# Second-layer modulation in half tiles, later stores of low parts, casts on ScalarE: a diffusion step on one core

## The chip, the core and the metric

The kernel runs on one core of a Trainium2 chip. The metric is device time in microseconds for one execution of the whole program. Engines are named as in the profile: TensorE (PE for matmuls, PEld for its weight loads), VectorE (DVE), ScalarE (ACT), GpSimd (POOL) and SyncE (SP), which issues the DMA transfers. PSUM is the memory into which TensorE accumulates, SBUF the working memory of all engines.

## What is computed

The reference is one inference step of a small diffusion backbone: two layers over 128 context tokens and 1024 latent tokens, 1024 features wide. Every layer normalises its input, scales and shifts it by a modulation computed from a conditioning vector, mixes tokens, adds the result back with a gate, and does the same once more around a feed-forward block with a 3-tap convolution. Layer 0 mixes by neighbourhood attention and pooling, layer 1 by a convolution module. Cut to what matters here:

```python
for i in range(DEPTH):                                        # 2 layers
    mc = jnp.split(sc @ w_mod[i] + b_mod[i], N_MOD, axis=-1)  # six vectors of 1024, context
    ml = jnp.split(sl @ w_mod[i] + b_mod[i], N_MOD, axis=-1)  # the same, latent
    hl = rmsnorm(xl, norm_mix[i]) * (1 + ml[1]) + ml[0]
    # even layer: attention + pooling, w_out;  odd layer: conformer_conv
    xl = xl + ml[2] * yl
    hl = rmsnorm(xl, norm_ffn[i]) * (1 + ml[4]) + ml[3]
    xl = xl + ml[5] * conv_ffn(hl, ffn_w_in[i], ffn_conv_w[i], ffn_conv_b[i], ffn_w_out[i])
```

Everything is float32. `w_mod[1]`, the second layer's modulation weights, is 1024 x 6144 numbers, 25 MB.

## The kernel before

Activations are kept feature-major: 128 features on the partitions, 1154 token columns (128 context, 2 of padding, 1024 latent). To keep float32 accuracy every matmul is done as three: weight and activation are each split into a rounded high part (`hi`, type float32r) and the rest (`lo`), and `mm3` (L254) adds hi·hi, hi·lo and lo·hi in PSUM (L259, L261, L263). The token axis is cut in two parts, A (about 664 columns, two PSUM banks) and B (about 492, one bank), which go through each stage one after the other, so that vector work of one part runs beside the matmuls of the other.

A weight unit of 128 x 1024 is brought in by `wload` (L233, one 512 KB DMA on SP into one of two `wraw` tiles) and split by `wunit` (L238): ScalarE makes `whi` by a rounding copy (L247), POOL subtracts to get `wlo` (L249). `whi` and `wlo` have three tiles each after attention. In the first FFN of layer 0 (part A) each low part is also stored to DRAM (L251, `lowi` and `lowo`, 66 stores), so that part B can load it (L246) instead of computing it again.

`norm` (L390) makes the modulated input of a stage: squares on ScalarE, sums on VectorE (L401), a column sum on TensorE (L375), a rsqrt on POOL (L366), a broadcast by TensorE (L387), then for each of 8 feature tiles a multiply on VectorE (L414), scale and shift on ScalarE (L416), the cast to the high part on VectorE (L422) and the low part on POOL (L423). With `halo` the first two columns are copied from the other part's tiles (L421, on VectorE). The same cast stands in `conv_norm` (L1048) and where the attention output is read back from DRAM for the output projection (L1281, 16 casts, the first of them before attention has ended). `norm` runs six times in the trunk, which makes 48 casts and 32 halo copies.

`mod_beside` (L304) computes the second layer's modulation on VectorE, beside matmuls of layer 0. For each of three thirds it goes over 16 chunks of 128 x 1024 weights (512 KB): one DMA on SP into the single tile `mraw` (L310, L311), then four multiply-accumulates of 512 columns (L319, for the first chunks L317), two for each half. The DMA waits until the tile's last reader is done. `keep_in_program_order` fixes the order among these. After 16 chunks a small matmul (L325) and `mod_spread` bring the result into place. The generator yields after each half; `trunk` pulls it four times (MS) after each output-projection tile of part A, and 1.1 times after each step of the first FFN. The residual add `x += gate * psum` (L432) evicts the output matmuls from PSUM on VectorE; in the FFN ScalarE (L1082) and VectorE (L1083, L1085) evict.

The order of instructions on each engine is fixed when the program is built, from a simulated timeline and the order of the program; on the chip each engine and each DMA queue then works strictly in that order. Transfers that the steps name: v rows are read back from DRAM in 128 loads (`vr`, L780), x and the attention output (`cat`) through SP as well.

```python
rv = raw[:, x * 512:(x + 1) * 512]                 # L313, in mod_beside: half of the one mraw tile
acc, c = accs[4 * s + 2 * u + x], self.sc[:, k, s:s + 1]
i = nc.vector.scalar_tensor_tensor(acc, rv, c, acc, op0=ALU.mult, op1=ALU.add)
```

Of the kernel before, what the change touches and what calls it, by code (L numbers as in the profile page):

```python
# [9 lines left out]
F32 = mybir.dt.float32  # L10
F32R = mybir.dt.float32r
AF = mybir.ActivationFunctionType
# [7 lines left out]
P = 128  # L20
# [11 lines left out]
H = 8  # L32
# [156 lines left out]
class Kern:  # L189
    def __init__(self, ctx, tc, ins, outs):  # L190
        self.tc = tc
        self.nc = tc.nc
        self.i = ins
        self.o = outs
        self.uid = 0
        self.pstack = None
        self.bg = []
        self.due = 0.0

    def nm(self, s):  # L200
# [32 lines left out]
    def wload(self, src):  # L233
        raw = self.wp.tile([P, 1024], F32, tag="wraw", name=self.nm("wraw"), bufs=2)
        self.nc.sync.dma_start(raw, src)
        return raw

    def wunit(self, src, raw=None, eng=None, keep=None, kept=None):  # L238

        nc = self.nc  # L240
        if raw is None:
            raw = self.wload(src)
        hi = self.wp.tile([P, 1024], F32R, tag="whi", name=self.nm("whi"), bufs=self.wbufs)
        lo = self.wp.tile([P, 1024], F32R, tag="wlo", name=self.nm("wlo"), bufs=self.wbufs)
        if kept is not None:
            nc.sync.dma_start(lo.bitcast(F32), kept)  # L246
        nc.scalar.activation(hi, raw, AF.Copy)  # L247
        if kept is None:
            (eng or nc.gpsimd).tensor_tensor(lo, raw, hi.bitcast(F32), op=ALU.subtract)  # L249
        if keep is not None:  # L250
            nc.sync.dma_start(keep, lo.bitcast(F32))  # L251
        return hi, lo

    def mm3(self, part, ps, whi, wlo, xhi, xlo, off, start, stop):  # L254
# [49 lines left out]
    def mod_beside(self, l, m, wp, ap, tag, ev):  # L304

        nc = self.nc
        accs = [ap.tile([P, UW], F32, tag=tag, name=self.nm("modacc"))[:, :512] for _ in range(8)]
        for k in range(KT):
            for u in range(2):
                raw = wp.tile([P, 1024], F32, tag="mraw", name=self.nm("mraw"), bufs=1)  # L310
                nc.sync.dma_start(raw, self.i["wmod"][l, m, k, :, u * 1024:(u + 1) * 1024])  # L311
                for x in range(2):
                    rv = raw[:, x * 512:(x + 1) * 512]  # L313
                    for s in range(2):
                        acc, c = accs[4 * s + 2 * u + x], self.sc[:, k, s:s + 1]
                        if k == 0:
                            i = nc.vector.tensor_scalar(acc, rv, c, None, op0=ALU.mult)  # L317
                        else:
                            i = nc.vector.scalar_tensor_tensor(acc, rv, c, acc, op0=ALU.mult, op1=ALU.add)  # L319
                        self.tc.keep_in_program_order(i)  # L320
                    yield
        ps = self.psa.tile([P, 512], F32, tag="aux", name=self.nm("modps"))
        for s in range(2):
            for g in range(4):
                nc.tensor.matmul(ps[32 * g:32 * g + 32, :], self.one[:, 1 - s:33 - s], accs[4 * s + g],  # L325
                                 start=s == 0, stop=s == 1)
        yield
        self.mod_spread(l, m, ps, ev, self.psa, "aux")
        yield
# [60 lines left out]
    def norm(self, part, xs, g, sh, H, tp, halo=None, gap=1):  # L390

        nc = self.nc
        W, c0, c1 = part.w, part.c0, part.c1
        acc = None
        for k in range(KT):
            sq = tp.tile([P, self.tw], F32, tag="ft", name=self.nm("sq"))
            nc.scalar.activation(sq[:, :W], xs[k][:, c0:c1], AF.Square)
            if acc is None:
                acc = sq
            else:  # L400
                nc.vector.tensor_tensor(acc[:, :W], acc[:, :W], sq[:, :W], op=ALU.add)  # L401
            yield
        ms = self.psa.tile([P, 512], F32, tag="aux", name=self.nm("ms"))
        st = part.toks()
        self.colsum(ms, (acc,), self.cst("on"), [o - c0 for o in st])
        r = self.rsqrt(ms[:, :len(st)], len(st))
        for _ in range(gap):
            yield
        rb = self.pstile()
        self.bcast(part, rb, r)  # L410
        off = c0 - H.base
        for k in range(KT):
            t = tp.tile([P, self.tw], F32, tag="ft", name=self.nm("nt"))
            nc.vector.tensor_tensor(t[:, :W], part.ps(rb), xs[k][:, c0:c1], op=ALU.mult)  # L414
            for s, a, b in part.streams(c0, c1):
                nc.scalar.activation(t[:, a - c0:b - c0], t[:, a - c0:b - c0], AF.Identity,  # L416
                                     bias=sh[:, k, s:s + 1], scale=g[:, k, s:s + 1])
            hi, lo = H.new()
            if halo is not None:
                for d, x in ((hi, halo.hi[k]), (lo, halo.lo[k])):  # L420
                    nc.vector.tensor_copy(d[:, 0:off], x[:, H.base - halo.base:c0 - halo.base])  # L421
            nc.vector.tensor_copy(hi[:, off:off + W], t[:, :W])  # L422
            nc.gpsimd.tensor_tensor(lo[:, off:off + W], t[:, :W], hi[:, off:off + W].bitcast(F32), op=ALU.subtract)  # L423
            H.hi.append(hi)
            H.lo.append(lo)
            yield
# [574 lines left out]
    def conv_norm(self, part, accs, H, sp, tp):  # L1001

        nc = self.nc
        A = part.c0 == 0
        W = part.w
        l0 = NCTX + CP
        sh = (lambda c: c if c < NCTX else c - L0 + l0) if A else (lambda c: c - part.c0)
        n = sh(part.c1 - 1) + 1
        st = [sh(c) for c in part.toks()]
        ms = self.psa.tile([P, 512], F32, tag="aux", name=self.nm("cmu"))  # L1010
        self.colsum(ms, (accs.pop(),), self.cst("on"), st)
        m = self.cp.tile([P, 24], F32, tag="mean", name=self.nm("mean"), bufs=1)
        nc.vector.tensor_copy(m[:, :len(st)], ms[:, :len(st)])
        for _ in range(NM):
            yield
        mb = self.pstile()
        self.bcast(part, mb, m)
        vs = None
        for k in range(KT):
            for _, pv, a, b in part.pieces(mb, part.c0, part.c1):  # L1020
                av = accs[k][:, sh(a):sh(a) + b - a]
                nc.vector.tensor_tensor(av, av, pv, op=ALU.subtract)
            sq = tp.tile([P, self.tw], F32, tag="ft", name=self.nm("csq"))
            nc.scalar.activation(sq[:, :n], accs[k][:, :n], AF.Square)
            if vs is None:
                vs = sq
            else:
                nc.gpsimd.tensor_tensor(vs[:, :n], vs[:, :n], sq[:, :n], op=ALU.add)
            yield
        ms = self.psa.tile([P, 512], F32, tag="aux", name=self.nm("cvar"))  # L1030
        self.colsum(ms, (vs,), self.cst("on"), st)
        r = self.rsqrt(ms[:, :len(st)], len(st))
        for _ in range(GC):
            yield
        rb = self.pstile()
        self.bcast(part, rb, r)
        for k in range(KT):
            t = tp.tile([P, self.tw], F32, tag="ft", name=self.nm("ct"))
            for _, pv, a, b in part.pieces(rb, part.c0, part.c1):
                av = accs[k][:, sh(a):sh(a) + b - a]  # L1040
                nc.vector.tensor_tensor(t[:, a - part.c0:b - part.c0], av, pv, op=ALU.mult)
            if A:
                nc.gpsimd.memset(t[:, NCTX:L0], 0.0)
            for _, a, b in part.streams(part.c0, part.c1):
                tv = t[:, a - part.c0:b - part.c0]
                nc.scalar.activation(tv, tv, AF.Silu, bias=self.par("lnb", k), scale=self.par("lng", k))
            hi, lo = H.new()
            nc.vector.tensor_copy(hi[:, :W], t[:, :W])  # L1048
            nc.gpsimd.tensor_tensor(lo[:, :W], t[:, :W], hi[:, :W].bitcast(F32), op=ALU.subtract)
            H.hi.append(hi)  # L1050
            H.lo.append(lo)
            yield
# [184 lines left out]
    def trunk(self):  # L1237
        tc, nc, I, cp = self.tc, self.nc, self.i, self.cp
# [10 lines left out]
        with ExitStack() as st:  # L1249
# [15 lines left out]
            for k in range(KT):  # L1265
                x = xp.tile([P, T], F32, name=f"x_{k}")
# [7 lines left out]
            for part, Hc in ((OA, mkA()), (OB, mkB(OB.c0))):  # L1274
                Hc.order = order
                tiles = {}
                for k in order:
                    c = ft.tile([P, self.tw], F32, tag="ft", name=self.nm("cat"))
                    nc.sync.dma_start(c[:, :part.w], self.cat[k][:, part.c0:part.c1])
                    hi, lo = Hc.new()  # L1280
                    nc.vector.tensor_copy(hi[:, :part.w], c[:, :part.w])  # L1281
                    nc.gpsimd.tensor_tensor(lo[:, :part.w], c[:, :part.w], hi[:, :part.w].bitcast(F32),
                                            op=ALU.subtract)
                    tiles[k] = (hi, lo)
# [207 lines left out]
```

## Time and profile before

| | |
|---|---|
| median of 3 runs | 2737.82 us (2730.47 to 2738.35) |
| the profiled execution | 2735.89 us, span of its trace 2734.1 us |
| mean granted TensorE clock | 0.986 |
| TensorE busy | 2643.0 us, 97% of the span |
| VectorE, ScalarE, POOL busy | 1690.7, 1071.8, 1265.3 us |
| DMA | 341 MB, 125 GB/s on average |

The span runs from the first to the last instruction; the execution's own time has 1.8 us around it. A busy TensorE is not one at its peak, as its matmuls overlap. The granted clock is the share of full speed that the chip let TensorE run at; it has two levels, 2.4 and 1.2 GHz. A row of a timeline gives start, duration, engine, line, operation and, in brackets, the engine's idle time before and what ended it.

### The profile page before, as it was taken

How to read it: one execution, taken by the hardware profiler on the slowest of the kernel's cores; microseconds unless marked ns; L12 is line 12 of the kernel's file. 1: busy time of each engine (PE TensorE's matmuls, PEld its weight loads, DVE VectorE, ACT ScalarE, POOL GpSimd, SP SyncE). 2: the span in 40 equal slices, each digit the busy share in tenths (PEclk: the TensorE clock that was granted, in tenths of full speed). 3: DMA queues.
4: the chain of work that ended last, by engine and by line, in shares of the span. 5: the costliest groups of instructions: out<-in, count | busy, mean ns of one | idle time of the engine just before them, and what ended most of it. 6: DMA issues, size and time to landing. Idle time of an engine off the chain costs nothing.

```text
span 2734.1 us, 38719 instructions
## 1 busy us (share of the span) xinstructions
PE 2643.0 (97%) x15108; PEld 2384.5 (87%) x15108; DVE 1690.7 (62%) x2568; ACT 1071.8 (39%) x1631; POOL 1265.3 (46%) x752
## 2 busy tenths in 40 slices
PE   8999998998999999999999999999999999999999
PEld 6688886787999988978999789989999999888887
DVE  3236878568666767764897864569965444544444
ACT  3325665523422222235555353455333322433332
POOL 1323444254423323215555253699756544645553
PEclk9999998998999999999999999999999999999999
DMA  7622224354445545644444554232222222433232
GB/s 264 198 75 68 55 54 131 124 181 138 153 149 193 184 163 171 201 161 141 144 145 133 177 172 135 74 99 70 66 82 70 78 79 76 123 93 93 93 94 91
DMA packets 130902, 341.16 MB, mean 125 GB/s; under 512 B 44960, under 2 KB 50208, under 8 KB 130720
## 3 DMA queue, kind: packets, MB, share of 16 engines
q1 hardware_dynamic: 130720, 338.68, 38.8%
q8 instruction: 120, 1.97, 0.3%
q14 instruction: 62, 0.51, 0.1%
HBM read 291.97 MB, written 46.67 MB: 124 GB/s over the span
## 4 chain that ended last, share of the span: by engine, by line
PE 75%; DVE 14%; DMA 7%; ACT 2%; issue 1%; POOL 1%; SPq 0%; POOLq 0%; DVEq 0%; ACTq 0%
PE mm L259 13%; PE mm L261 13%; PE mm L263 13%; PE mn L259 8%; PE mn L261 7%; PE mn L263 7%; DMA mraw<-in_wmod_dram 4%; DVE modacc L319 4%; PE mm L449 2%; DVE x L432 1%; DVE dacc L987 1%; PE O L879 1%; PE ms L479 1%; PE qps L629 1%; PE qps L631 1%
## 5 line engine op out<-in xcount | busy, mean ns | idle before, releaser
L249 POOL TENSOR_TENSOR wlo<-wraw,whi 128x1024 fp32r<-128x1024 f32 x280 | 686.9, 2458 | 915.1 <-ACT whi L247 767.2
L247 ACT ACTIVATE whi<-wraw 128x1024 fp32r<-128x1024 f32 x348 | 364.5, 1056 | 763.7 <-PE mm L261 374.8
L259 PE MATMUL mm<-h,whi 128*128 128x332 f32 (+6 forms) x2208 | 558.5, 324 | 9.2 <-DVE x L432 8.7
L263 PE MATMUL mm<-h,wlo 128*128 128x332 f32 (+6 forms) x2208 | 559.9, 324 | 0.1
L261 PE MATMUL mm<-h,whi 128*128 128x332 f32 (+6 forms) x2208 | 559.5, 324 | 0.0
L259 PEld LDWEIGHTS mm<-h,whi 128*128 128x128 f32 x2208 | 382.5, 189 | 22.5 <-issue 10.4
L263 PEld LDWEIGHTS mm<-h,wlo 128*128 128x128 f32 x2208 | 381.2, 189 | 12.7 <-issue 0.8
L261 PEld LDWEIGHTS mm<-h,whi 128*128 128x128 f32 x2208 | 379.8, 189 | 11.0 <-issue 0.8
L987 DVE SCALAR_TENSOR_TENSOR dacc<-u,params,dacc 128x661 f32<-128x661 f32 (+1 forms) x344 | 285.4, 830 | 7.5
L432 DVE SCALAR_TENSOR_TENSOR x<-mm,mod,x 128x128 f32<-128x128 f32 (+7 forms) x408 | 210.7, 560 | 101.0 <-PE mm L263 87.1
L259 PE MATMUL mn<-h,whi 128*128 128x494 f32 (+1 forms) x672 | 262.8, 391 | 2.9 <-DVE x L432 2.9
L261 PE MATMUL mn<-h,whi 128*128 128x494 f32 (+1 forms) x672 | 262.3, 390 | 0.0
L263 PE MATMUL mn<-h,wlo 128*128 128x494 f32 (+1 forms) x672 | 260.8, 390 | 0.0
L319 DVE SCALAR_TENSOR_TENSOR modacc<-mraw,sc,modacc 128x512 f32<-128x512 f32 x168 | 167.8, 1053 | 67.5 <-DMA mraw<-in_wmod_dram 67.5
L1083 DVE SCALAR_TENSOR_TENSOR facc<-mm,params,facc 128x663 f32<-128x663 f32 (+3 forms) x92 | 81.9, 891 | 206.2 <-ACT facc L1082 206.0
L1083 DVE SCALAR_TENSOR_TENSOR facc<-mn,params,facc 128x493 f32<-128x493 f32 (+1 forms) x84 | 62.0, 738 | 207.8 <-ACT facc L1082 207.7
L259 PE MATMUL mm<-fh,whi 128*128 128x332 f32 (+2 forms) x720 | 173.5, 321 | 15.7 <-DVE x L432 13.3
L263 PE MATMUL mm<-fh,wlo 128*128 128x332 f32 (+2 forms) x720 | 171.5, 318 | 0.3 <-POOL wlo L249 0.3
L261 PE MATMUL mm<-fl,whi 128*128 128x332 f32 (+2 forms) x720 | 171.6, 318 | 0.0
L969 POOL TENSOR_TENSOR acc<-acc,tap 128x508 f32<-128x508 f32 (+1 forms) x104 | 151.1, 1455 | 38.0 <-ACT tap L968 31.8
L432 DVE SCALAR_TENSOR_TENSOR x<-mn,mod,x 128x510 f32<-128x510 f32 (+1 forms) x168 | 120.6, 737 | 64.7 <-PE mn L263 64.1
L1095 POOL TENSOR_TENSOR facc<-facc,facc 128x494 f32<-128x494 f32 (+2 forms) x66 | 91.2, 1382 | 149.9 <-DVE facc L1085 149.9
(227 smaller groups left out, 4555.6 us busy)
## 6 DMA issues: line engine op xcount, KB each, us to landing
wraw<-in_fi_dram SPq DMA_DIRECT2D x176, 512.0 KB
mraw<-in_wmod_dram SPq DMA_DIRECT2D x96, 512.0 KB
wraw<-in_fo_dram SPq DMA_DIRECT2D x88, 512.0 KB
wraw<-in_pw_dram SPq DMA_DIRECT2D x48, 512.0 KB
lowi<-wlo SPq DMA_DIRECT2D x44, 512.0 KB
wlo<-lowi SPq DMA_DIRECT2D x44, 512.0 KB
lowo<-wlo SPq DMA_DIRECT2D x22, 512.0 KB
wlo<-lowo SPq DMA_DIRECT2D x22, 512.0 KB
```

Of the source, the lines that this page charges most:

```text
L247: nc.scalar.activation(hi, raw, AF.Copy)
L249: (eng or nc.gpsimd).tensor_tensor(lo, raw, hi.bitcast(F32), op=ALU.subtract)
L259: mm(pv, whi, xhi[:, a:b], start=start, stop=False)
L261: mm(pv, whi, xlo[:, a:b], start=False, stop=False)
L263: mm(pv, wlo, xhi[:, a:b], start=False, stop=stop)
L319: i = nc.vector.scalar_tensor_tensor(acc, rv, c, acc, op0=ALU.mult, op1=ALU.add)
L432: nc.vector.scalar_tensor_tensor(xd[:, a:b], pv, gate[:, d, st:st + 1], xd[:, a:b], op0=ALU.mult, op1=ALU.add)
L449: mm(ps[:, c, :n], w[:, s], x[k][:, o:o + n], start=a, stop=b)
L969: nc.gpsimd.tensor_tensor(acc[:, :n], acc[:, :n], p[:, :n], op=ALU.add)
L987: nc.vector.scalar_tensor_tensor(acc[:, :n] if t == NCK - 1 else pacc, u[:, t:t + n], wk(i, t), acc[:, :n] if t == side else pacc, op0=ALU ...
L1083: nc.vector.scalar_tensor_tensor(acc[:, 1:W], part.ps(ps, 0, W - 1), w(0), acc[:, 1:W], op0=ALU.mult, op1=ALU.add)
L1095: (nc.gpsimd if side or part.n == 1 else nc.vector).tensor_tensor(a[:, :W], a[:, :W], g[:, :W], op=ALU.mult)
```

## The change

Four edits. The modulation loads of `mod_beside` become halves of 128 x 512 (256 KB), each with its own DMA into one of three tiles. A low part is no longer stored by `wunit` itself: the store is noted and issued by the next `wload`, behind that load. The casts to the high part in `norm`, `conv_norm` and the read-back of the attention output, and the halo copies in `norm`, go from VectorE to ScalarE. Arithmetic and results stay the same.

```diff
@@ Kern.__init__
+        self.stores = []
@@ wload
         raw = self.wp.tile([P, 1024], F32, tag="wraw", name=self.nm("wraw"), bufs=2)
         self.nc.sync.dma_start(raw, src)
+        for dst, lo in self.stores:
+            self.nc.sync.dma_start(dst, lo)
+        self.stores = []
         return raw
@@ wunit
         if keep is not None:
-            nc.sync.dma_start(keep, lo.bitcast(F32))
+            self.stores.append((keep, lo.bitcast(F32)))
@@ mod_beside
-                raw = wp.tile([P, 1024], F32, tag="mraw", name=self.nm("mraw"), bufs=1)
-                nc.sync.dma_start(raw, self.i["wmod"][l, m, k, :, u * 1024:(u + 1) * 1024])
                 for x in range(2):
-                    rv = raw[:, x * 512:(x + 1) * 512]
+                    rv = wp.tile([P, 512], F32, tag="mraw", name=self.nm("mraw"), bufs=3)
+                    o = u * 1024 + x * 512
+                    nc.sync.dma_start(rv, self.i["wmod"][l, m, k, :, o:o + 512])
@@ norm
-                    nc.vector.tensor_copy(d[:, 0:off], x[:, H.base - halo.base:c0 - halo.base])
-            nc.vector.tensor_copy(hi[:, off:off + W], t[:, :W])
+                    nc.scalar.activation(d[:, 0:off], x[:, H.base - halo.base:c0 - halo.base].bitcast(F32), AF.Copy)
+            nc.scalar.activation(hi[:, off:off + W], t[:, :W], AF.Copy)
@@ conv_norm
-            nc.vector.tensor_copy(hi[:, :W], t[:, :W])
+            nc.scalar.activation(hi[:, :W], t[:, :W], AF.Copy)
@@ trunk
-                    nc.vector.tensor_copy(hi[:, :part.w], c[:, :part.w])
+                    nc.scalar.activation(hi[:, :part.w], c[:, :part.w], AF.Copy)
```

## Rows read from the trace of the kernel before

**Rows 1.** The page, part 1: busy time, share of the span, instructions.

```profile
PE 2643.0 (97%) x15108; PEld 2384.5 (87%) x15108; DVE 1690.7 (62%) x2568; ACT 1071.8 (39%) x1631; POOL 1265.3 (46%) x752
```

**Rows 2.** Stretches: busy us (x instructions) of PE, PEld, DVE, ACT, POOL; PEclk; DMA.

```profile
440.00:480.00 40.00, 29.82 (x176) 18.32 (x176) 35.24 (x60) 18.20 (x45) 26.23 (x18) 0.79 0.62 193
605.00:665.00 60.00, 44.42 (x182) 37.61 (x181) 47.20 (x53) 14.73 (x20) 28.38 (x14) 0.83 0.40 132
665.00:1190.00 525.00, 509.95 (x3246) 493.15 (x3245) 369.69 (x501) 154.59 (x182) 177.14 (x77) 0.99 0.52 172
1190.00:2734.00 1544.00, 1524.21 (x8243) 1369.32 (x8241) 925.74 (x1264) 620.25 (x775) 854.53 (x507) 1.00 0.34 107
```

**Rows 3.** Waits of TensorE from 535 to 665 us: total, times, longest.

```profile
PE mm L259 <- DVE x L432: 8.7, 3, 5.2
PE mm L387 <- POOL rsr L366: 5.0, 1, 5.0
PE ms L375 <- DVE sq L401: 4.1, 1, 4.1
```

**Rows 4.** Timeline of SP: start us, us, what it issues.

```profile
623.36 0.33 SPq L311 DMA_DIRECT2D mraw<-in_wmod_dram  x1
...
630.29 0.33 SPq L311 DMA_DIRECT2D mraw<-in_wmod_dram  x1
```

**Rows 5.** Timeline of VectorE: start us, us, what [idle before, releaser].

```profile
609.99 6.93 DVE L319 SCALAR_TENSOR_TENSOR modacc<-mraw,sc,modacc 128x512 f32<-128x512 f32 x4 [2.01 <-DMA mraw<-in_wmod_dram]
...
627.52 2.74 DVE L319 SCALAR_TENSOR_TENSOR modacc<-mraw,sc,modacc 128x512 f32<-128x512 f32 x4 [3.55 <-DMA mraw<-in_wmod_dram]
630.18 0.72 DVE L432 SCALAR_TENSOR_TENSOR x<-mm,mod,x 128x490 f32<-128x490 f32 x1
```

**Rows 6.** Timeline of TensorE, output projection, part B: the same columns.

```profile
625.03 0.38 PE L263 MATMUL mm<-h,wlo 128*128 128x490 f32 x1
625.25 0.38 PE L259 MATMUL mm<-h,whi 128*128 128x490 f32 x1
...
657.58 0.75 PE L259 MATMUL mm<-h,whi 128*128 128x490 f32 x1 [5.18 <-DVE x L432]
```

**Rows 7.** Waits from 665 to 1190 us: SP's first, then other engines'.

```profile
SPq L251 <- POOL wlo L249: 235.8, 48, 13.6
SPq L311 <- DVE modacc L319: 135.7, 30, 9.0
...
ACT whi L247 <- DMA wraw<-in_fi_dram: 61.6, 8, 11.9
...
PE mm L259 <- DVE x L432: 9.4, 5, 3.8
```

**Rows 8.** Timeline at the end of attention: VectorE, then TensorE.

```profile
451.31 1.80 DVE L1281 CAST h<-cat 128x664 fp32r<-128x664 f32 x1
...
453.63 0.55 PE L847 MATMUL tp<-consts,prob 128*128 128x128 f32 x3 [2.08 <-DVE prob L731]
```

**Rows 9.** The chain in order of time: start us, us, what.

```profile
297.34 2.25 DMA vr<-vd
```

**Rows 10.** The page, part 6, loads of v rows: count, KB each.

```profile
vr<-vd SPq DMA_DIRECT2D x128, 32.0 KB
```

**Rows 11.** Groups of instructions: busy us, mean ns, idle before; VectorE, then ScalarE.

```profile
L319 DVE SCALAR_TENSOR_TENSOR modacc<-mraw,sc,modacc 128x512 f32<-128x512 f32 x168 | 167.8, 1053 | 67.5 <-DMA mraw<-in_wmod_dram 67.5
...
L422 DVE CAST h<-nt 128x664 fp32r<-128x664 f32 (+3 forms) x48 | 48.9, 1039 | 5.3 <-ACT nt L416 5.2
...
L1048 DVE CAST h<-ct 128x648 fp32r<-128x648 f32 (+1 forms) x16 | 18.0, 1143 | 1.4 <-ACT ct L1046 1.4
...
L1281 DVE CAST h<-cat 128x664 fp32r<-128x664 f32 (+1 forms) x16 | 13.3, 839 | 8.2 <-DMA cat<-cat 8.2
...
L421 DVE CAST h<-h 128x2 fp32r<-128x2 f32 x32 | 11.4, 389 | 2.1 <-PE mm L261 1.7
...
L1098 ACT ACTIVATE fh<-facc 128x664 fp32r<-128x664 f32 (+3 forms) x88 | 60.3, 685 | 254.7 <-POOL facc L1095 148.1 <-DVE facc L1095 106.5
```

## The prediction, made before the changed kernel ran

> **What bounds the kernel now.** I read the page's engine table first: TensorE is busy 97% of the span, VectorE 62%, ScalarE 39% [rows 1]. So time can be won only where TensorE idles or runs at the lower of its two clock levels, and the next view, the stretches, shows where that is [rows 2]. From 605 to 665 us it idles 60 - 44.4 = 15.6 us at a mean granted clock of 0.83: 60 x 0.17 x 2 = 20 us at 1.2 GHz. At that level a matmul takes twice as long, so half of the busy part of it, 20 x 0.74 / 2 = 7.5 us, is lost as well: 23 us. In the first FFN, 665 to 1190 us, 15.0 us idle and by the same sum (clock 0.99) about 5 more: 20 us. At the end of attention, 440 to 480 us, 10.2 us idle and 0.79 of the clock, 6 more: 16 us. The 1544 us after that idle 20 us in all. The three stretches hold 59 us.
>
> Third view, who waits for whom from 535 to 665 us: TensorE waits for VectorE's residual adds (L432), 8.7 us in three waits, for the square sum of the norm, 4.1, and for its rsqrt, 5.0 [rows 3]. Fourth, the queues in order of time. SP issues a 512 KB modulation load at 623.36 and the next at 630.29 us, 6.9 us apart, because there is one tile for it and SP waits until VectorE is done with it [rows 4]. VectorE then sits 3.55 us, runs four accumulations in 2.74 us and only then the next residual add, which is queued behind them [rows 5]. One residual add thus leaves every 6.9 us. TensorE starts a matmul of 490 columns each 0.22 us at the full level, so a tile of 24 costs it 5.3 us; it runs out of PSUM and stops, 5.18 us at 657.58 [rows 6]. This stretch goes at the pace of the modulation loads, not of matmuls.
>
> In the first FFN SP loses 235.8 us to stores of low parts that wait for the subtraction on POOL (L251) and 135.7 us to modulation loads that wait for VectorE (L311). Behind both stand the weight loads, and ScalarE waits 61.6 us for `fi` weights, with the PSUM evictions (L1082) behind it. TensorE's longest cause there is again L432, 9.4 us [rows 7]. In attention a cast (mean of its line 0.84 us [rows 11]) took 1.80 us at 451.31 and held VectorE's next softmax step; TensorE waited 2.08 us for that step [rows 8].
>
> **The change part by part.** *Modulation in halves, three tiles.* It removes 48 loads of 512 KB and adds 96 of 256 KB, 48 more issues of 0.33 us on SP [rows 4], 16 us over some 640 us in which SP mostly waits: nothing, as long as SP runs ahead. The landing of 256 KB is not in the trace. Lower bound 2.25 us, a 32 KB load [rows 9, 10]; upper bound the 512 KB load, 623.36 to 627.52 = 4.2 us [rows 4, 5]. I take 3.1, half way, since a quarter megabyte lies half way in size. A tile then cycles in 0.33 + 3.1 + two accumulations of 0.75 = 4.9 us, and three tiles give a half each 1.6 us, against 1.5 us of VectorE's own work: no wait. At 4.2 us the half comes each 2.0 us. A full unit with its residual add takes then at most 4.0 + 0.7 = 4.7 us, below the 5.3 us of the matmul tile. So from 605 to 665 us the pace becomes TensorE's. Of the 23 us I take back 17. About 6 stay with the norm's own chain of square sum and rsqrt, which waited 9.1 us [rows 3] and whose steps on three engines remain. Bounds: 8 (the waits for L432 alone) to 23.
>
> *First FFN.* The same lead removes the DMA part of VectorE's queue, and the low-part store no longer stands ahead of the next weight load. The store is not cheaper and not fewer; it waits less, as its subtraction is done when SP reaches it, and the load it is moved past needs only the older of two tiles. Behind it on SP stand the next modulation half and weight load; both gain. A low-part tile is held up to one unit longer, which three tiles cover at 5.3 us of matmuls a unit or more. Of 20 us I take back 12, since the accumulations themselves stay and four in a row can still delay an eviction. Bounds 4 and 20.
>
> *Casts and halo copies on ScalarE.* VectorE loses 48.9 + 18.0 + 13.3 + 11.4 = 92 us of instructions that last 0.4 to 1.1 us on average [rows 11]. ScalarE gets 80 casts at the 0.685 us of its own rounding copy L1098 [rows 11], 55 us, and 32 halo copies, which I price at the 0.389 us they took on VectorE, 12 us: 67 us on an engine idle for over half the span. In the norms the cast follows ScalarE's own scale step, so one hop between engines goes. In attention the eight casts of that stretch leave the queue in which softmax waits: the 2.08 us gap [rows 8] and some of the clock behind it. I take 4 us, bounds -11 (16 casts of 0.685, all on the chain through ScalarE) and 16.
>
> *Elsewhere* (six norms, the convolution): the rows after 1190 us hold 20 us of idle time [rows 2], little of it near a cast. 0, bounds -5 and +5.
>
> Sum: 17 + 12 + 4 = 33 us off the profiled execution's 2735.9 us: 2703. That execution lies 1.9 us under the median of 2737.8, so in medians 2705 us.
>
> **Rivals.** *The port, not the load (slower gain).* The accumulation took 1.05 us on average, though four undisturbed ones take 2.74 us; beside a subtraction on POOL four took 6.93 us [rows 5, 11]. If those set the pace once the loads are early, a unit needs up to 6.9 + 0.7 us where POOL is at work and the residual adds stay late in part: 9 instead of 17 us, 5 instead of 12, and 4: 18 us, 2720. For it: mean against undisturbed. Against: from 605 to 665 us POOL is busy 28.4 of 60 us [rows 2], so most accumulations run undisturbed. The Trainium skill, SBUF — State Buffer, section Who interferes with whom, states the rule behind this: a VectorE instruction with two SBUF inputs and a GpSimd instruction that reads SBUF shut each other out for a whole instruction. By that rule the accumulations stay as slow as they are, wherever the casts go; the 6.93 us agree with it.
>
> *The lead does not come about.* SP issues in order; if a weight load that waits for its tile stands ahead of the modulation halves, VectorE still waits. Then 4 us in each of the three parts, 12: 2726. For it: SP loses over 370 us to waits in the first FFN [rows 7]. Against: from 605 to 665 us the weight load goes out right behind each modulation load, so it has no wait of its own.
>
> *ScalarE's queue takes over (slower).* Place: casts in front of weight splits, softmax and PSUM evictions. Price: the 67 us added. With 33 us won, the kernel gets slower by over 0.3% (8 us, about what a measurement here tells from no change) from the point where (33 + 8) / 67 = 61% of it reaches TensorE; at 70% it is 47 - 33 = 14 slower, 2752. For it: ScalarE already waits 61.6 us for loads with evictions behind [rows 7]. Against: 39% busy [rows 1].
>
> *More comes free:* all 59 us but some 8 of the norm's chain, 51: 2687.
>
> **How the numbers follow.** Forecast 0.55 (own range 2694 to 2716), port 0.16, no lead 0.12, ScalarE 0.11, more 0.06. Faster (below 2729.6): 0.55 + 0.16 + 0.06 and a third of the no-lead case, 0.81. Within 0.3%: the other two thirds, 0.08. Slower 0.11. The range runs from 2686, the largest gain, to 2729, which takes in the port and part of the no-lead case and leaves out some 2 in 10.
>
> **What would show it.** Right: VectorE's wait for `mraw`, 67.5 us [rows 11], nearly gone; modulation loads up to three ahead; from 605 to 665 us a residual add each 5 to 5.5 us and a clock near 1.00; L251 gone from the longest waits of SP; ScalarE near 1140 us busy, VectorE near 1600. Wrong: the four accumulations still at 5 us or more with TensorE waiting for L432 (port); VectorE still waiting for `mraw` (no lead); TensorE waiting for weight splits, softmax or evictions behind casts on ScalarE (slower).

## The result, and the profile after

The changed kernel took 2717.55 us (median of 4 runs, 2716.47 to 2722.01) against 2736.14 us for the kernel before beside it: a ratio of 0.9938, 95% interval 0.9915 to 0.9961. It is faster by 0.6%, 18.6 us, where 2705 us (33 us off) was forecast; it lies in the stated range of 2686 to 2729, just above the forecast's own range (2694 to 2716), at 56% of the predicted gain.

The page's engine table of the kernel after, beside [rows 1]:

```profile
PE 2635.2 (97%) x15108; PEld 2379.8 (88%) x15108; DVE 1605.9 (59%) x2456; ACT 1122.9 (41%) x1743; POOL 1260.9 (46%) x752
```

VectorE lost 85 us and ScalarE gained 51. The trace shows more of each part. The groups of accumulations (L324 is the former L319) and of the moved casts, after; columns as in [rows 11]:

```profile
L324 DVE SCALAR_TENSOR_TENSOR modacc<-mraw,sc,modacc 128x512 f32<-128x512 f32 x168 | 158.4, 992 | 0.1
```

```profile
L427 ACT ACTIVATE h<-nt 128x664 fp32r<-128x664 f32 (+3 forms) x48 | 31.5, 675 | 0.2
...
L1286 ACT ACTIVATE h<-cat 128x664 fp32r<-128x664 f32 (+1 forms) x16 | 10.8, 682 | 11.7 <-DMA cat<-cat 11.6
...
L1053 ACT ACTIVATE h<-ct 128x648 fp32r<-128x648 f32 (+1 forms) x16 | 10.6, 674 | 0.0
...
L426 ACT ACTIVATE h<-h 128x2 fp32r<-128x2 f32 x32 | 5.6, 196 | 7.6 <-PE mm L266 7.3
```

VectorE's wait for `mraw`, 67.5 us before, is 0.1 us: the lead is there. The casts take 0.68 us each and the halo copies 0.20, 58.5 us in all where 67 were priced.

Both programs issue 15108 matmuls, and the boundaries of the stages fall on the same numbers in all traces below. So the time at which a given matmul starts splits a trace into stages. In us, with the start of the output projection's part A at matmul 3018, part B at 3402 and the first FFN at 3620. The column "first FFN" is cut at matmul 6500, some 75 us before that FFN's part A is done (matmul 6924); "rest" runs from 6500 to the start of the last matmul:

```
                    to 2500   attention's   part A   part B   first FFN   rest
                              end, to 3018
before                435.7       98.7        61.7     68.5      461.4    1602.2
after                 437.0      100.6        62.3     60.0      450.5    1600.8
after - before         +1.3       +1.9        +0.6     -8.5      -10.9      -1.4
```

The gain of 17 us between the two traces comes from part B and the first FFN (up to matmul 6924 the FFN gains 10.1 us, 535.5 to 525.4). How far single traces differ can be seen where the programs are alike: up to matmul 2500 all traces of this study take 432.6 to 438.2 us. The stretches of the kernel after, beside [rows 2]:

```profile
605.00:665.00 60.00, 50.59 (x231) 43.43 (x230) 38.01 (x46) 29.13 (x55) 38.45 (x18) 0.91 0.47 145
665.00:1190.00 525.00, 513.25 (x3293) 498.20 (x3292) 347.12 (x490) 160.28 (x189) 169.13 (x74) 0.99 0.52 173
```

From 605 to 665 us TensorE still idles 9.4 us (15.6 before) at a mean granted clock of 0.91 (0.83). From 535 to 665 us it waits longer for residual adds than before (11.5 us against 8.7 [rows 3]), and hardly for the norm's rsqrt (0.8 against 5.0):

```profile
PE mm L264 <- DVE x L437: 11.5, 5, 3.8
PE mm L392 <- POOL rsr L371: 0.8, 1, 0.8
```

The timeline of VectorE there shows what took the loads' place:

```profile
585.00 4.54 DVE L324 SCALAR_TENSOR_TENSOR modacc<-mraw,sc,modacc 128x512 f32<-128x512 f32 x2
589.46 1.02 DVE L437 SCALAR_TENSOR_TENSOR x<-mm,mod,x 128x128 f32<-128x128 f32 x2
...
595.98 2.73 DVE L324 SCALAR_TENSOR_TENSOR modacc<-mraw,sc,modacc 128x512 f32<-128x512 f32 x4
598.63 1.02 DVE L437 SCALAR_TENSOR_TENSOR x<-mm,mod,x 128x128 f32<-128x128 f32 x2
599.58 5.05 DVE L324 SCALAR_TENSOR_TENSOR modacc<-mraw,sc,modacc 128x512 f32<-128x512 f32 x4
604.55 0.84 DVE L406 TENSOR_TENSOR sq<-sq,sq 128x664 f32<-128x664 f32 x1
605.31 2.73 DVE L324 SCALAR_TENSOR_TENSOR modacc<-mraw,sc,modacc 128x512 f32<-128x512 f32 x4
607.96 1.02 DVE L437 SCALAR_TENSOR_TENSOR x<-mm,mod,x 128x128 f32<-128x128 f32 x2
```

No idle time stands in brackets any more: from 558 to 630 us VectorE works without a pause. But between the residual adds (L437) of 589.46, 598.63 and 607.96 us lie 9.2 and 9.3 us, full of eight accumulations each, and a tile of part A asks TensorE for 62.3 / 8 = 7.8 us with its stalls, of part B for 5.3. TensorE still stops for them, here at the beginning of part B:

```profile
599.80 0.47 PE L264 MATMUL mm<-h,whi 128*128 128x490 f32 x1 [1.64 <-DVE x L437]
...
609.12 0.46 PE L264 MATMUL mm<-h,whi 128*128 128x490 f32 x1 [3.79 <-DVE x L437]
...
618.25 0.46 PE L264 MATMUL mm<-h,whi 128*128 128x490 f32 x1 [2.02 <-DVE x L437]
...
627.87 0.75 PE L264 MATMUL mm<-h,whi 128*128 128x490 f32 x1 [2.85 <-DVE x L437]
```

In the first FFN a new pattern stands four times (at 856, 902, 1089 and 1135 us, the last behind matmul 6500): six accumulations of three tiles ahead of a residual add, at 856 and 1089 us in a row, at 902 and 1135 with one other instruction of 0.84 us among them. First VectorE, then TensorE and then SP, kernel after:

```profile
850.99 4.06 DVE L324 SCALAR_TENSOR_TENSOR modacc<-mraw,sc,modacc 128x512 f32<-128x512 f32 x6
854.97 2.90 DVE L437 SCALAR_TENSOR_TENSOR x<-mm,mod,x 128x128 f32<-128x128 f32 x6
```

```profile
856.14 0.54 PE L264 MATMUL mm<-fh,whi 128*128 128x332 f32 x2 [2.05 <-DVE x L437]
```

```profile
847.71 11.84 SPq L318 DMA_DIRECT2D mraw<-in_wmod_dram  x5
```

SP issues five halves as the tiles come free, VectorE runs the six accumulations, and the residual add behind them is late by 2.05 us for TensorE. The stores, finally, wait as long as before. SP's waits over the whole span, kernel after (L238 is the store in its new place, L318 the modulation load):

```profile
SPq L238 <- POOL wlo L254: 241.0, 53, 13.7
...
SPq L318 <- DVE modacc L324: 180.8, 80, 9.0
```

That is 241.0 us at the store, 242.5 before in its old place (235.8 of them in the first FFN [rows 7]).

### The profile page after: what moved, and what is told of

Read it like the earlier page. It is cut to its first block, busy times and chain, and to the rows that moved or that the text cites. A ratio compares the mean times of both kernels' runs of the same rounds, so it can differ in the third digit from the quotient of the medians.

```text
span 2716.6 us, 38806 instructions
## 1 busy us (share of the span) xinstructions
PE 2635.2 (97%) x15108; PEld 2379.8 (88%) x15108; DVE 1605.9 (59%) x2456; ACT 1122.9 (41%) x1743; POOL 1260.9 (46%) x752
## 4 chain that ended last, share of the span: by engine, by line
PE 80%; DVE 12%; DMA 3%; ACT 3%; issue 1%; POOL 1%; SPq 0%; POOLq 0%; DVEq 0%; ACTq 0%
PE mm L264 14%; PE mm L266 14%; PE mm L268 14%; PE mn L264 7%; PE mn L266 7%; PE mn L268 7%; DVE modacc L324 2%; DVE dacc L992 2%; PE mm L454 2%; DVE x L437 2%; PE O L884 1%; PE ms L484 1%; PE tp L852 1%; PE qps L634 1%; PE qps L636 1%
## 5 line engine op out<-in xcount | busy, mean ns | idle before, releaser
L264 PE MATMUL mm<-h,whi 128*128 128x332 f32 (+6 forms) x2208 | 559.0, 324 | 11.5 <-DVE x L437 11.5
L437 DVE SCALAR_TENSOR_TENSOR x<-mm,mod,x 128x128 f32<-128x128 f32 (+7 forms) x408 | 210.4, 561 | 128.3 <-PE mm L268 126.4
L324 DVE SCALAR_TENSOR_TENSOR modacc<-mraw,sc,modacc 128x512 f32<-128x512 f32 x168 | 158.4, 992 | 0.1
L437 DVE SCALAR_TENSOR_TENSOR x<-mn,mod,x 128x510 f32<-128x510 f32 (+1 forms) x168 | 120.5, 737 | 63.7 <-PE mn L268 62.9
```

The source lines that it names most:

```text
L264: mm(pv, whi, xhi[:, a:b], start=start, stop=False)
L437: nc.vector.scalar_tensor_tensor(xd[:, a:b], pv, gate[:, d, st:st + 1], xd[:, a:b], op0=ALU.mult, op1=ALU.add)
```

## The experiments

The theory to be tested: the early loads gave the whole gain, and what is missing of the forecast is VectorE's own work, the accumulations packed into part A. Rivals: the stores gave the first FFN's share; the casts gave it by freeing VectorE. All stage times below are read from the traces as in the table above; ratios are against the kernel before on the same chip. Three of the traces have three tiles and pulls as changed (after, runs 1 and 4): their part B takes 57.6 to 60.0 us, their first FFN 450.5 to 451.7, which shows how well a stage repeats.

**1 to 3: one edit alone.** Each is the kernel before with one of the three hunks of the change: the halves (1), the stores (2), all casts and halo copies (3).

> Only the modulation in halves with three tiles; stores and casts as before. Theory 1 (the 18 us came from the loads being early, in the output projection and in the first FFN): 13 to 17 us faster than before, and VectorE's wait for mraw falls from 67.5 us to under 5. Theory 2 (the first FFN's share, 10 us by the count of matmuls, came from the later stores): about 8 us faster. Theory 3 (VectorE's freed 92 us of casts gave the gain): under 5 us faster.

> Only the stores of low parts one unit later. Theory 1: within 3 us of before, although SP's 242 us at L251 go. Theory 2: 8 to 10 us faster, all of it in the first FFN (matmul 4000 to 6500 of the trace). Theory 3: within 3 us of before.

> Only the casts and halo copies on ScalarE. Theory 1: within 4 us of before, with attention (up to matmul 3000) about 3 us later as in the changed kernel. Theory 2: the same. Theory 3: 8 to 15 us faster, as VectorE loses some 85 us of work.

```
                 median us   ratio [95% interval]       att. end  part A  part B  first FFN   rest
1 halves          2716.24    0.9926 [0.9908, 0.9945]      99.3     64.0    58.6     451.7    1604.0
2 stores          2734.82    0.9991 [0.9980, 1.0003]      97.0     63.2    67.2     462.8    1600.1
3 casts           2733.50    0.9993 [0.9978, 1.0008]     101.5     60.2    67.2     461.4    1596.8
```

The halves alone give all of it, by the ratio 20 us, a little more than the 13 to 17 expected; the stores and the casts alone change nothing that can be measured. The accumulations of run 1 wait 0.0 us for their loads:

```profile
L319 DVE SCALAR_TENSOR_TENSOR modacc<-mraw,sc,modacc 128x512 f32<-128x512 f32 x168 | 154.7, 969 | 0.0
```

Run 2 shows why the stores gave nothing. SP's wait at the store, and ScalarE's for `fi` weights (total, times, longest):

```profile
SPq L238 <- POOL wlo L253: 248.0, 50, 13.7
```

```profile
ACT whi L251 <- DMA wraw<-in_fi_dram: 85.2, 18, 11.9
```

The wait only changed its place in the queue (242.5 us before, 248.0 now), and ScalarE's wait for `fi` weights stayed (83.8 us before over the whole span, 85.2 now). The subtraction on POOL is not done when SP comes to the store one load later; TensorE, 462.8 us in the first FFN, does not feel it either way. In run 3 VectorE lost 75 us of work, and up to matmul 6500 the first FFN did not get shorter by a tenth of a microsecond; attention's end got 2.8 us longer, part A and part B 1.5 and 1.3 us shorter, the rest 5 us shorter.

**4: the 16 casts of the read-back attention output on VectorE again.**

```diff
-                    nc.scalar.activation(hi[:, :part.w], c[:, :part.w], AF.Copy)
+                    nc.vector.tensor_copy(hi[:, :part.w], c[:, :part.w])
```

> The changed kernel with the casts of the read-back attention output on VectorE again (16 casts); norm, conv_norm, halves and stores as changed. If these 16 casts on ScalarE cost attention its 3 us (matmul 3000 came at 534.6 instead of 531.5 us): matmul 3000 back at 531 to 532 us and the whole 2 to 4 us faster than the changed kernel, about 2714. If the shift is only another order of the end of attention: matmul 3000 anywhere between 530 and 536 us, and the whole within 2 us of the changed kernel.

2715.58 us, ratio 0.9923 [0.9907, 0.9940]: 2 us under the changed kernel, not apart from it by the intervals. In the trace attention's end is back at 98.7 us (100.6 changed); matmul 3000 came at 529.6 us, 1.9 us before the kernel before, which had been so since matmul 2500. Over all traces of this study with unchanged work up to there, attention's end took 96.9 to 99.3 us with these casts on VectorE (before, runs 1, 2, 4, 9, 10, 11) and 100.0 to 102.0 us with them on ScalarE (after, runs 3, 5, 7, 8). So on ScalarE they cost attention's end some 3 us, as expected. Part A takes it back: 59.1 to 62.3 us with the casts on ScalarE, 61.7 to 64.0 with them on VectorE. Both stages together took 159.1 to 163.0 us with them on ScalarE and 160.1 to 163.3 on VectorE, so the place of these casts does not show in the sum.

**5: the accumulations spread over both parts.** MS is the number of halves pulled after each step of the output projection in part A, MT the same for part B. Part A has 6 steps, not 8, as its first takes three tiles at once, and part B has 8. So 4 and 0 pull 24 halves, 2 and 2 pull 28. In the traces 48 accumulations start between matmuls 3018 and 3620 in the kernel after (25 in part A, 23 in part B) and 44 in run 5 (20 and 24); the rest of the 56 ran in the first FFN.

```diff
-MS = 4
-MT = 0
+MS = 2
+MT = 2
```

> The changed kernel with the pulls of the modulation spread over both parts of the output projection (MS = 2, MT = 2 instead of 4 and 0). Theory 1 (with the loads early, the 60 odd accumulations packed into part A of the output projection keep VectorE busy without a gap from 558 to 630 us, residual adds queue behind them, and that took back some 13 us of what the prediction counted on): part B (matmuls 3402 to 3620, 60.0 us in the changed kernel, 46.6 us at TensorE's own pace) falls to 48 to 53 us and the whole is 6 to 12 us faster than the changed kernel, about 2708. Rival (what is left there is the norm's own chain of sums, rsqrt and broadcast): part B stays within 3 us of 60 and the whole within 3 us of the changed kernel.

2706.84 us, ratio 0.9889 [0.9869, 0.9909], some 11 us under the changed kernel. Part A 59.1, part B 52.4 us (62.3 and 60.0 in the changed kernel); the first FFN 452.4. The stretch from 605 to 665 us, run 5:

```profile
605.00:665.00 60.00, 55.74 (x285) 50.10 (x284) 52.94 (x54) 28.29 (x55) 38.44 (x17) 0.94 0.50 164
```

TensorE idles 4.3 us instead of 9.4. The theory holds, although the accumulations packed there were 48 and not the 60 odd of the expectation: part B lost 7.6 us with about as many accumulations in it (24 against 23). What changed is how many stand ahead of a residual add, four instead of eight. The rival of the norm's own chain does not hold for those 7.6 us, as the norm did not change; of what is left, 3.9 us are TensorE's wait for the norm's rsqrt.

**6: POOL taken away.** In `wunit`, for the 16 output projection units of layer 0 only:

```diff
+        if not sub:
+            nc.scalar.activation(hi, raw, AF.Copy)
+            return hi, hi
```

> The changed kernel without the subtraction of the low parts for the 16 output projection units of layer 0; the high part is used in their place, so the low part of that weight is left out of the result. If the accumulations are slow because POOL works beside them (992 ns on average against 747 undisturbed), those before 640 us fall from some 1.15 us to under 0.9 us on average and part B (matmuls 3402 to 3620) loses 6 to 12 of its 60.0 us. If POOL has no part in it, they stay above 1.05 us and part B stays within 3 us of 60.

2694.48 us, ratio 0.9844 [0.9821, 0.9868]. Part B takes 45.2 us, without a wait of TensorE. The accumulations of 535 to 640 us, first in the kernel after, then in run 6 (VectorE's busy time is the third of the pairs):

```profile
535.00:640.00 105.00, 0.00 (x0) 0.00 (x0) 55.04 (x48) 0.95 0.59 196
```

```profile
535.00:640.00 105.00, 0.00 (x0) 0.00 (x0) 37.03 (x48) 1.00 0.65 221
```

55.04 / 48 = 1.15 us each beside POOL, 37.03 / 48 = 0.77 without. The accumulations are slow because POOL works at the same time. This pair of rows agrees with the rule of the Trainium skill, SBUF — State Buffer, section Who interferes with whom, which the prediction weighed; the last section shows it record by record. A rival for part B's gain, that POOL's emptier queue lets the norm's rsqrt come sooner, has little room: TensorE waited 0.8 us for it in the kernel after, and part B lost 14.8. The run also frees attention's end of three subtractions (95.4 us), so its whole is no measure of the port alone.

**7 and 8: two tiles, one tile.** The changed kernel with another number of half tiles:

```diff
-                    rv = wp.tile([P, 512], F32, tag="mraw", name=self.nm("mraw"), bufs=3)
+                    rv = wp.tile([P, 512], F32, tag="mraw", name=self.nm("mraw"), bufs=2)
```

and `bufs=1`.

> The changed kernel with two half tiles instead of three. Theory 1 (the lead does it): by the sum of the prediction (0.33 + 3.1 + 1.5 = 4.9 us for a tile's cycle) two tiles give a half each 2.5 us, so VectorE waits for mraw again, 20 to 40 us in all, but TensorE loses only 0 to 4 us against the changed kernel. Rival (bursts: three tiles let six accumulations run in a row ahead of a residual add, which cost TensorE four waits of 2.05 us in the first FFN): those four waits go and the first FFN (matmuls 4000 to 6500, 393.1 us) gets 3 to 8 us shorter.

> The changed kernel with one half tile. If the lead and not the smaller piece is what gained: each half costs a full landing with nothing beside it, VectorE's wait for mraw rises above the 67.5 us of before (96 landings of some 3 us, half of them uncovered: 100 to 200 us), and the whole is 0 to 15 us slower than before. If the smaller piece alone gains: at least 8 us faster than before.

```
                 median us   ratio [95% interval]       att. end  part A  part B  first FFN   rest
7 two tiles       2712.37    0.9908 [0.9885, 0.9932]     102.0     61.0    66.2     443.7    1595.4
8 one tile        2785.31    1.0177 [1.0150, 1.0204]     101.1     59.8    72.5     497.6    1610.2
```

One half tile is much slower than one whole tile: the lead is what gains, not the smaller piece. (Two whole tiles of 512 KB were not tried.) It missed its expectation on the far side (49 us slower, 0 to 15 expected), as the first FFN lost 36 us up to matmul 6500 and 46 up to 6924. Its waits over the span show it:

```profile
DVE modacc L324 <- DMA mraw<-in_wmod_dram: 133.0, 61, 5.0
...
PE mm L264 <- DVE x L437: 52.6, 13, 8.6
```

Two tiles bring the waits for `mraw` to 14.8 us, fewer than the 20 to 40 expected, and as the bursts theory said the four waits of 2.05 us in the first FFN go; it gets 6.8 us shorter up to matmul 6500, which has three of the four. Part B gets 6.2 us longer: TensorE waits 9.1 us there for the norm's rsqrt, which comes late, and up to 6.0 us for a residual add.

**9: the kernel before, spread.** MS = 2 and MT = 2 without any part of the change.

> The kernel before with only the pulls spread (MS = 2, MT = 2). Theory 1 (with one 512 KB tile the loads set the pace, wherever the accumulations are pulled): both parts of the output projection together (130.2 us before, 122.3 changed, 111.5 changed and spread) stay above 125 us, and the whole is within 6 us of before. Rival (spreading alone does it, the early loads are not needed): below 118 us and at least 10 us faster than before.

2722.96 us, ratio 0.9958 [0.9940, 0.9975]. Both parts together take 63.2 + 64.7 = 127.9 us, above 125 as theory 1 had it, but the whole is 11 us faster by the ratio, nearly twice what it allowed: the first FFN took 453.8 us instead of 461.4. Part B needs the lead and the spreading both (52.4 us in run 5); the first FFN gains from either. Why the FFN does so here was not tried.

**10 and 11: what beats both.** The changed kernel with run 5's MS and MT and run 4's casts (10), and with two tiles as well (11).

> The changed kernel with MS = 2, MT = 2 and the 16 casts of the read-back attention output on VectorE. If those casts cost attention 2 to 3 us on ScalarE, this is 2 to 4 us faster than the spread kernel (2706.8), about 2704, and matmuls 2500 to 3018 take 97 to 99 us instead of 100.0. If not: within 2 us of 2706.8.

> As the run before, with two half tiles instead of three. Bursts theory (three tiles let six accumulations stand in a row ahead of a residual add in the first FFN): the first FFN (from matmul 3620 to 6500, 452.4 us in the spread kernel, 443.7 with two tiles and pulls as changed) falls to 442 to 447 us, the whole is about 2697 to 2700. Rival (the shorter FFN of the two-tile kernel came from work left over or a stall moved into the output projection, 61.0 + 66.2 us there): what the FFN gains the output projection loses again, and the whole stays within 3 us of the three-tile run beside it.

```
                 median us   ratio [95% interval]       att. end  part A  part B  first FFN   rest
10                2705.36    0.9899 [0.9874, 0.9924]      97.1     63.2    52.4     450.9    1597.0
11                2697.42    0.9865 [0.9836, 0.9894]      97.1     63.2    49.1     443.3    1598.0
```

Against run 5, run 10 wins 2.9 us at the end of attention and loses 4.1 in part A, where the second eight casts now stand in VectorE's queue; the time does not move by more than the intervals. Run 11 is 20 us under the changed kernel. The first FFN falls to 443.3 us, and part B does not pay for it: spread out, two tiles are lead enough. Its stretches, beside [rows 2]:

```profile
605.00:665.00 60.00, 56.47 (x312) 51.44 (x311) 53.73 (x56) 29.69 (x58) 36.31 (x17) 1.00 0.53 173
665.00:1190.00 525.00, 521.36 (x3316) 501.64 (x3315) 337.21 (x491) 167.50 (x199) 175.04 (x77) 1.00 0.52 177
```

TensorE idles 3.5 us of 60 and 3.6 of 525, both at a granted clock of 1.00.

## Why the prediction was right, and by how much it was not

**Right:** the bound. TensorE lost its time to residual adds behind accumulations that waited for one tile's load; the lead removed that wait (67.5 us to 0.1), and runs 1 and 8 show that it made the whole gain. Of the signs named beforehand, the wait for `mraw` and the busy time of VectorE (1605.9 us) came as forecast; the clock near 1.00 from 605 to 665 us (0.91) and the store's wait leaving SP's longest did not. The landing of 256 KB was put at 3.1 us. With one half tile the load issued at 595.14 us is used at 598.09 and that of 622.79 at 626.37: 3.0 and 3.6 us with the issue. Run 8, SP and VectorE:

```profile
595.14 0.33 SPq L318 DMA_DIRECT2D mraw<-in_wmod_dram  x1
...
622.79 0.33 SPq L318 DMA_DIRECT2D mraw<-in_wmod_dram  x1
```

```profile
598.09 2.62 DVE L324 SCALAR_TENSOR_TENSOR modacc<-mraw,sc,modacc 128x512 f32<-128x512 f32 x2 [2.22 <-DMA mraw<-in_wmod_dram]
...
626.37 1.42 DVE L324 SCALAR_TENSOR_TENSOR modacc<-mraw,sc,modacc 128x512 f32<-128x512 f32 x2 [2.96 <-DMA mraw<-in_wmod_dram]
```

**Output projection: 17 us forecast, 7.9 measured** (130.2 to 122.3 us in both parts). The step that failed is the sentence that a full unit with its residual add takes at most 4.7 us, below the matmul tile's 5.3. It set one unit of four accumulations against a tile of part B, at 0.75 us each. In the trace before, four stood between two residual adds, each group waiting for its load. Once the loads were early, they stood where the program pulls them, eight to a step of part A (MS = 4), at 1.15 us each on average beside POOL. The argument that most would run undisturbed was right and did not help: of the 48, 33 took at most 0.76 us, and the 15 others held 33.9 of the 57.7 us that the 48 add up to (55.0 as busy time, since neighbours overlap a little). In the timeline above eight of them took 5.05 + 2.73 = 7.8 us, a square sum 0.84 and the residual add 1.02: 9.6 us with small overlaps, 9.3 from one residual add to the next, where the tile's matmuls need 7.8 or 5.3. VectorE became the bound. Run 5 shows it by placing, run 6 by taking POOL away; either brings part B to or near TensorE's pace. The 6 us that the prediction left to the norm's chain were not what stayed: that was 11.5 us at residual adds and 0.8 at the rsqrt.

**First FFN: 12 us forecast, 10.9 measured** (10.1 up to matmul 6924). The size was right and half of the reason wrong. The claim that the store waits less, since its subtraction is done when SP reaches it, failed: 241.0 us against 242.5, and run 2 alone gains nothing. The lead did it (run 1: 451.7 us), and more would have come without the bursts of six accumulations that the third tile allows (run 7: 443.7).

**Casts: 4 us gain forecast, none measured.** Attention's end got 1.9 us longer. The queue in which softmax waits did get free: from 440 to 535 us TensorE waited 7.7 us for VectorE's softmax steps and scaled queries (`prob`, `st`, `qs`) before and 2.2 after. The step that failed is to count that wait alone. The casts entered ScalarE's queue, which also copies the transposed probabilities to their high part (L856); the low part (L857, on VectorE) follows that copy, and TensorE's waits for it grew from 5.4 to 10.3 us, after and then before:

```profile
PE O L879 <- DVE ptl L857: 6.5, 4, 2.8
PE O L884 <- DVE ptl L857: 3.8, 3, 2.3
```

```profile
PE O L879 <- DVE ptl L852: 3.2, 4, 1.7
PE O L874 <- DVE ptl L852: 2.2, 2, 1.6
```

In run 4, with these casts on VectorE again, the same wait is 4.9 us. ScalarE after shows a cast that waits for its read-back (11.6 us in all in front of L1286) with such a copy behind it:

```profile
443.92 0.76 ACT L1286 ACTIVATE h<-cat 128x664 fp32r<-128x664 f32 x1 [0.87 <-DMA cat<-cat]
444.59 0.58 ACT L856 ACTIVATE pth<-tp 128x512 fp32r<-128x512 f32 x1
```

What attention's end lost, part A won back (run 4). The 75 us that VectorE lost in run 3 bought nothing (0.9993). **Elsewhere:** 0 forecast, -1.4 behind matmul 6500 and +1.3 up to matmul 2500, no more than single traces differ.

Of the rivals, the port's number (2720) was nearest to the time, and its mechanism is real (run 6). Part of that nearness is luck: it stood for 9 and 5 and 4 us, and measured were 7.9, 10.9 and -1.9. The no-lead case and ScalarE as the bound did not occur.

## What to carry to other kernels

When a wait in an in-order queue goes, ask where the work behind it will run next, not only how fast: work that late data had spread out falls back to the place where the program puts it, and may become the bound there. Prefetch depth and placement belong together; here two tiles and an even spread (run 11) beat three tiles and a packed one by 20 us. Moving a store behind the next load gained nothing here, as the subtraction it waited for was no earlier; moving copies to another engine only moved the wait.

## What was not expected of the hardware

Two accumulations of 512 columns, undisturbed 1.5 us, took 4.54 us at 585.00 us, while POOL subtracted from 582.67 to 589 us without a pause. The timeline of POOL, kernel after, and then the two accumulations by themselves, from narrower windows of VectorE's timeline:

```profile
582.67 3.51 POOL L1287 TENSOR_TENSOR h<-cat,h 128x490 fp32r<-128x490 f32 x2
586.14 2.85 POOL L254 TENSOR_TENSOR wlo<-wraw,whi 128x1024 fp32r<-128x1024 f32 x1
```

```profile
585.00 1.73 DVE L324 SCALAR_TENSOR_TENSOR modacc<-mraw,sc,modacc 128x512 f32<-128x512 f32 x1
586.65 2.88 DVE L324 SCALAR_TENSOR_TENSOR modacc<-mraw,sc,modacc 128x512 f32<-128x512 f32 x1
```

The first ends at 586.73 us, 0.55 after POOL's second subtraction (586.18), the other at 589.53, 0.54 after its third (588.99). The whole trace shows the same: of the 168 accumulations of L324, 143 take at most 0.76 us and 25 take 1.1 to 2.9, and each of these 25 ends 0.55 us after the end of a subtraction on POOL. An accumulation is not slowed a little by POOL: it runs at full speed, or it is held until the subtraction that it met is over. The average over a stage (1.15 us against 0.77, a factor of 1.5) hides that.
